# A new order for a diffusion backbone's first loads and first products

## The chip, the cores and the metric

The kernel runs on one core of a Trainium2 chip. A core has a matrix engine (TensorE, PE in the profile; its weight loads are listed as PEld), three engines for elementwise work (VectorE or DVE, ScalarE or ACT, GpSimd or POOL) and a sync engine (SyncE or SP), whose queue issues all loads and stores here. Each engine works through its own list of instructions in order, and they wait for one another through semaphores. The metric is the device time of one execution, in microseconds (us).

## The reference

Two layers over 1024 latent tokens of a 64-wide grid and 256 context tokens, all of width 1024, in float32. Each layer takes a modulation (shift, scale and gate for two halves of the layer) from a conditioning vector, normalizes and modulates the tokens, and mixes them. Cut to what the change touches, the head of layer 0:

```python
ml = (silu(c) @ w_mod[0] + b_mod[0]).reshape(B, 6, 1, D)      # for the latent tokens
mc = (silu(c_ctx) @ w_mod[0] + b_mod[0]).reshape(6, D)         # for the context tokens
hl = rms_norm(xl) * (1.0 + ml[:, 1]) + ml[:, 0]
hc = rms_norm(xc) * (1.0 + mc[1]) + mc[0]
pl, pc = hl @ w_in, hc @ w_in                                  # 1024 -> 1184 columns
```

Behind it come latent attention with low-rank queries and keys, a multi-scale pooling, an out-projection and a convolutional feed-forward; then layer 1 with grouped-query attention, its own feed-forward, and a last normalization of the latent stream.

## The kernel before, in words

Everything is held transposed: the feature on the 128 partitions, the token along the row. Tokens come in three chunks: 0 and 1 are the latent tokens 0 to 511 and 512 to 1023, chunk 2 the 256 context tokens. A chunk has eight feature tiles, k = 0 to 7. A product of accuracy near float32 is made from three products of a rounded high part and a low part (high x high, high x low, low x high), in mm3 (L72).

The head of the program, L505 to L708, is a region in which the order is written out by hand for all five engines: within one engine the instructions run in the order of the calls. It consists of small helpers that the change reorders:

- load_x(c) loads a chunk of tokens: eight tiles of 256 KB for chunks 0 and 1 (L445, L441), four for chunk 2 (L436). Tiles 0 to 3 of chunk 1 go into the buffers of chunk 0's tiles 0 to 3, and its tiles 4 to 7 into those of modulation weights that have been used.
- load_mod(n, half) loads eight tiles of 256 KB of the modulation's weights: n = 0 is the shift, n = 1 the scale; half 0 is feature tiles 0 to 3, half 1 is 4 to 7. g00, g10, g01 and g11 are (0,0), (1,0), (0,1) and (1,1).
- mod_rows(g) multiplies the conditioning vectors with one such half: eight float32 products of 512 columns on TensorE (L460), each two passes, then a copy of the resulting row on ScalarE (L462). mod_turn turns the row into columns with four tiny transposes on TensorE (L469), and two VectorE steps add the bias (L473).
- squares(xs, n) and add_squares: per tile a Square on ScalarE (L184 the first, L187 the others) and an addition on VectorE (L188); squares then splits the sum into a high part (ScalarE, L195) and a low part (VectorE, L196). total (L203, L204) adds them over the partitions on TensorE. newton makes the norm factor r of it: three steps of ScalarE (L167, L169, L170), and in the function that it returns three of VectorE (L173 to L175).
- scaled(c, k, r) multiplies a tile by r (VectorE, L477). high(c, k) makes the modulated high part on ScalarE (L487) and a float32 copy on GpSimd (L488), low_(c, k) the low part on VectorE (L489).
- getw(i) loads the i-th block of in-projection weights, 512 KB (L96); split(mt) makes its high part (GpSimd L117, or ScalarE L115) and its low part (VectorE, L111). The first three are blocks 4, 5 and 6, keys and part of the queries. The load buffers are two, and the first holds a row of srow until it is stored to d_sil.
- some(mt, c, k) is one call of mm3 for block mt, chunk c and tile k: three products. evac(mt, c) copies the finished sum out (ScalarE, L408).

So every engine's order in this stage is the order of these calls. Behind the region the buffers of the tokens are freed and the next stage begins (L907), written out by hand too except for SyncE. The change ends about halfway through the region; from high(2, 2) on they are the same.

Of the kernel before, what the change touches and what calls it, by code (L numbers as in the profile page):

```python
# [15 lines left out]
D = 1024  # L16
# [28 lines left out]
def backbone(tc, a):  # L45
# [161 lines left out]
    def rms_of(sq, n, width, tmp, psb, dst):  # L207

        newton(sq[0], total(sq, n, psb), n, width, tmp, dst)()
# [73 lines left out]
    def tables(name, pinned=True):  # L283

        i = S.preload_act_table_set(name)
        if pinned:
            tc.keep_in_program_order(i)
# [98 lines left out]
    def getw(i, **kw):  # L386
        if i < len(order) and order[i] not in win:
            win[order[i]] = wload(a["win0"][order[i]], **kw)

    def split(mt):  # L390
        if mt in win and callable(win[mt]):
            win[mt] = win[mt](mt not in (4, 5, 6), packed=mt == 9)

    prows = {}

# [33 lines left out]
    def load_x(c):  # L429
        c0, n = CH[c]  # L430
        xin[c] = []
        for k in range(8):
            if k % 2 == 0:
                if c == 2:
                    t2 = xp.tile([128, 512], F32, name="xin", tag="xin", bufs=4)
                    dma.dma_start(t2, a["xc"][:, k : k + 2, :])  # L436
                elif c == 0 or k < 4:
                    t2 = row(k // 2 % 2, name="xin")
            if c == 1 and k > 3:
                xin[c].append(hp.tile([128, 512], F32, name="xin", tag="h", bufs=40))  # L440
                dma.dma_start(xin[c][k], a["xl"][k, :, c0 : c0 + n])  # L441
                continue
            t = t2[:, k % 2 * n : k % 2 * n + n]
            if c < 2:
                dma.dma_start(t, a["xl"][k, :, c0 : c0 + n])  # L445
            xin[c].append(t)

    def load_mod(n, half):

        res = []  # L450
        for k in range(8):
            res.append(hp.tile([128, 512], F32, name="wn", tag="h", bufs=40))
            dma.dma_start(res[-1], a["wmodn"][n, half, k])
        return res

    def mod_rows(ws):

        b = psb("mod")[:2]
        for k in range(8):
            PE.matmul(b, scol[:, k, :], ws[k], start=k == 0, stop=k == 7)  # L460
        t = tmp("mrow", 512)[:2]
        S.copy(t, b)  # L462
        return t
# [11 lines left out]
    def scaled(c, k, r):  # L475

        V.tensor_mul(xin[c][k], xin[c][k], r)  # L477
# [24 lines left out]
    def low_(c, k):  # L502
        lows[c, k]()
# [8 lines left out]
    S.activation(scol, scol, AF.Silu)  # L512
    S.activation(srow, srow, AF.Silu)
    tables("natural_log_exp_and_others", False)
    g00 = load_mod(0, 0)
    load_x(0)
    g10 = load_mod(1, 0)
    dma.dma_start(d_sil, srow)
    dma.dma_start(ident, a["ident"])
    dma.dma_start(bmod, a["bmod"])  # L520
    r0 = tmp("r", 512)
    sq = squares(xin[0], 512, tmp, V)
    t0 = mod_rows(g00)
    g01 = load_mod(0, 1)
    rms_of(sq, 512, D, tmp, psb, r0)
    scaled(0, 3, r0)
    scaled(0, 7, r0)
    scaled(0, 0, r0)
    scaled(0, 5, r0)
    scaled(0, 1, r0)  # L530
    t1 = mod_rows(g10)
    getw(0)
    getw(1)
    mod_turn(0, 0, t0, 0.0)
    scaled(0, 6, r0)
    mod_turn(1, 0, t1, 1.0)
    g11 = load_mod(1, 1)
    high(0, 0)
    low_(0, 0)
    high(0, 1)  # L540
    split(4)
    split(5)
    scaled(0, 2, r0)
    low_(0, 1)
    high(0, 2)
    low_(0, 2)
    scaled(0, 4, r0)
    high(0, 3)
    low_(0, 3)
    t2 = mod_rows(g01)  # L550
    dma.dma_start(convw, a["convw"])
    some(4, 0, 0)
    some(4, 0, 1)
    getw(2, p=xp, tag="w", bufs=1)
    load_x(2)
    load_x(1)
    some(5, 0, 0)
    some(4, 0, 3)
    sq2 = squares(xin[2], 256, tmp, V)
    some(5, 0, 1)  # L560
    split(6)
    some(5, 0, 3)
    acc = add_squares(xin[1][:4], 512, tmp, V)
    mod_turn(0, 1, t2, 0.0)
    t3 = mod_rows(g11)
    some(5, 0, 2)
    r2 = tmp("r", 256)
    ss2 = total(sq2, 256, psb)
    rest2 = newton(sq2[0], ss2, 256, D, tmp, r2)
    r1 = tmp("r", 512)  # L570
    dma.dma_start(cols, a["cols"])
    some(6, 0, 0)
    mod_turn(1, 1, t3, 1.0)
    high(0, 5)
    high(0, 4)
    some(4, 0, 2)
    some(6, 0, 2)
    high(0, 7)
    some(6, 0, 1)
    low_(0, 5)  # L580
    some(6, 0, 3)
    some(4, 0, 5)
    low_(0, 4)
    some(5, 0, 4)
    rest2()
    high(0, 6)
    some(5, 0, 5)
    low_(0, 7)
    some(6, 0, 4)
    sq1 = squares(xin[1][4:], 512, tmp, V, acc)  # L590
    some(4, 0, 4)
    scaled(2, 7, r2)
    scaled(2, 5, r2)
    some(6, 0, 5)
    low_(0, 6)
    scaled(2, 6, r2)
    ss1 = total(sq1, 512, psb)
    some(6, 0, 6)
    scaled(2, 1, r2)
    rest1 = newton(sq1[0], ss1, 512, D, tmp, r1)  # L600
    high(2, 1)
    scaled(2, 4, r2)
    some(6, 0, 7)
    some(5, 0, 6)
    scaled(2, 2, r2)
    some(5, 0, 7)
    evac(6, 0, bk[6, 0])
    scaled(2, 0, r2)
    high(2, 0)
    rest1()  # L610
    evac(5, 0, bk[5, 0])
    some(4, 0, 6)
    some(4, 0, 7)
    high(2, 2)
    low_(2, 0)
    scaled(2, 3, r2)
# [2578 lines left out]
```

## Time and profile before

| What | Value |
|---|---|
| Runs | 2889.85 us median of 3 (2889.62 to 2891.6) |
| Profiled execution | 2893.38 us in all, span 2891.4 us |
| Granted TensorE clock over the span | 0.989 of full speed |
| TensorE busy, 40 to 50 us / 60 to 70 us / 80 to 90 us | 7.67 / 6.73 / 8.78 of 10 us |
| VectorE busy, 60 to 70 us | 8.94 of 10 us |
| ScalarE busy, 20 to 30 us / 30 to 40 us | 2.18 / 3.85 of 10 us |
| Bytes loaded, 10 to 20 us | 382 GB/s |

In a timeline each line is one instruction or several merged ones: start, time that they took together, engine, source line, operation, output<-input, sizes, count, and in brackets how long the engine sat idle before it and what ended that. The start and end of matrix products are modelled, so a product's listed time is longer than the step from one to the next. A row with 1.00 as clock (PEclk) had TensorE at full speed.

### The profile page before, as it was taken

To read this page: it belongs to the slowest core of one execution; us is meant where nothing else is said; L and a number is where in the kernel's file an instruction comes from. 1 tells how busy PE (TensorE), PEld (TensorE's weight loads), DVE (VectorE), ACT (ScalarE), POOL (GpSimd) and SP (SyncE) were. 2 spreads that over 40 slices of the span, in tenths; PEclk is the share of its full clock that TensorE was granted. 3 is DMA by queue.
4 is the path that set the end of the run, shared out by engine and by line. 5 is a ranking of instruction groups with operands and counts; after the bars stand their busy time and mean duration, and the time that the engine had idled before them with its cause. 6 is when DMAs were issued, how large, how long until landed. Compare 5 with 4: busy or idle time off the path is not lost.

```text
span 2891.4 us, 40143 instructions
## 1 busy us (share of the span) xinstructions
PE 2781.4 (96%) x14654; PEld 2316.9 (80%) x14654; DVE 2214.3 (77%) x3646; ACT 1240.3 (43%) x2520; POOL 1072.3 (37%) x1066
## 2 busy tenths in 40 slices
PE   7988999999999999999999998999999999999997
PEld 3857888887887888888888777999877788887886
DVE  5688888879887777778777887888757666559766
ACT  5525888824422333332002445888634333333104
POOL 2242444762243455431012443444331445452112
PEclk9999999999999999999999999999999999999998
DMA  6144001283144343363221010000131222226311
GB/s 229 70 141 139 15 24 58 81 277 110 55 130 127 108 137 128 131 209 125 73 72 49 31 37 23 1 1 1 37 138 44 81 88 73 85 93 228 98 59 59
DMA packets 97229, 264.89 MB, mean 92 GB/s; under 512 B 11908, under 2 KB 21060, under 8 KB 96904
## 3 DMA queue, kind: packets, MB, share of 16 engines
q1 hardware_dynamic: 97032, 262.33, 27.1%
q8 instruction: 115, 1.88, 0.3%
q14 instruction: 82, 0.67, 0.1%
HBM read 212.53 MB, written 49.75 MB: 91 GB/s over the span
## 4 chain that ended last, share of the span: by engine, by line
PE 58%; DVE 10%; ACT 3%; issue 2%; DMA 1%; POOL 1%; DVEq 0%; SPq 0%; ACTq 0%; POOLq 0%
PE d L72 18%; PE y L72 9%; PE x L72 6%; PE z L72 6%; PE p L72 5%; PE pv L1277 3%; PE b L72 3%; PE T L1264 2%; PE S L1197 1%; PE S L1199 1%; PE S L1198 1%; PE qk L72 1%; DVE x L2009 1%; DVE x L2008 1%; DMA wm<-in_wmod 1%
## 5 line engine op out<-in xcount | busy, mean ns | idle before, releaser
L2091 DVE SCALAR_TENSOR_TENSOR x<-d,mod,x 128x512 f32<-128x512 f32 (+1 forms) x352 | 254.5, 735 | 94.8 <-PE d L72 92.5
L1246 POOL TENSOR_SCALAR p<-p,sm 128x1280 f32<-128x1280 f32 x128 | 171.4, 1339 | 287.9 <-DVE sm L1245 190.2
L1267 DVE TENSOR_TENSOR tl<-T,th 128x512 fp32r<-128x512 f32 x328 | 225.5, 688 | 46.8 <-ACT th L1266 41.8
L1277 PE MATMUL pv<-th,v 128*128 128x256 f32 x976 | 254.1, 309 | 1.4 <-ACT vo L1406 1.0
L1220 DVE TENSOR_REDUCE mx<-S 128x1 f32<-128x512 f32 (+1 forms) x400 | 233.9, 585 | 11.0 <-PE S L1199 3.7
L72 PE MATMUL d<-act,wh 128*128 128x512 f32 (+1 forms) x832 | 231.9, 365 | 0.0
L1266 ACT CAST th<-T 128x512 fp32r<-128x512 f32 x328 | 192.1, 586 | 84.5 <-PE T L1264 77.2
L2074 ACT CAST act<-act 128x512 fp32r<-128x512 f32 (+1 forms) x110 | 61.3, 577 | 382.2 <-PE d L72 259.8
L72 PE MATMUL b<-h,wh 128*128 128x512 f32 (+1 forms) x752 | 206.6, 362 | 6.0 <-DVE h L489 4.1
L1694 POOL TENSOR_TENSOR x<-raw 128x512 f32<-128x512 f32 x80 | 114.5, 1432 | 237.2 <-DMA raw<-in_wup 158.7
L72 PE MATMUL x<-h,a1h 128*128 128x512 f32 x624 | 197.7, 398 | 2.5 <-ACT a1h L1676 2.5
L1264 PE MATMUL T<-ident,p 128*128 128x128 f32 x1280 | 193.0, 272 | 1.5 <-POOL p L1246 1.5
L1975 ACT COPY su<-x 128x512 f32<-128x512 f32 x40 | 23.4, 586 | 381.4 <-PE x L72 348.7
L1264 PEld LDWEIGHTS T<-ident,p 128*128 128x128 f32 x1280 | 156.5, 140 | 34.9 <-POOL p L1246 3.2
L1277 PE MATMUL pv<-tl,v 128*128 128x256 f32 x656 | 177.3, 282 | 0.0
L1277 PEld LDWEIGHTS pv<-th,v 128*128 128x128 f32 x976 | 173.4, 189 | 2.4 <-ACT vo L1406 1.5
L72 PEld LDWEIGHTS d<-act,wh 128*128 128x128 f32 x832 | 149.5, 189 | 27.2
L2015 POOL TENSOR_TENSOR su<-x,su 128x512 f32<-128x512 f32 x78 | 140.5, 1813 | 79.5 <-DVE su L1997 67.0
L72 PEld LDWEIGHTS b<-h,wh 128*128 128x128 f32 x752 | 133.0, 189 | 36.0 <-DVE h L489 5.4
L72 PE MATMUL d<-act,wl 128*128 128x512 f32 (+1 forms) x416 | 151.9, 365 | 0.0
L72 PEld LDWEIGHTS x<-h,a1h 128*128 128x128 f32 x624 | 118.6, 190 | 30.3 <-ACT a1h L1676 2.9
L1237 ACT ACTIVATE p<-S,mx,rq 128x512 f32<-128x512 f32 (+1 forms) x192 | 136.2, 712 | 12.6 <-DVE mx L1228 11.1
(515 smaller groups left out, 8185.0 us busy)
## 6 DMA issues: line engine op xcount, KB each, us to landing
raw<-in_wup SPq DMA_DIRECT2D x86, 512.0 KB, 3.3
wm<-in_wmod SPq DMA_DIRECT2D x72, 512.0 KB, 3.6
act<-d_act SPq DMA_DIRECT2D x88, 256.0 KB, 3.5
raw<-in_wdn SPq DMA_DIRECT2D x44, 512.0 KB, 4.3
raw<-in_wout SPq DMA_DIRECT2D x32, 512.0 KB, 3.4
d_act<-su SPq DMA_DIRECT2D x22, 640.0 KB, 3.4
d_act<-su SPq DMA_DIRECT2D x22, 512.0 KB, 2.9
raw<-in_win SPq DMA_DIRECT2D x20, 512.0 KB, 3.5
```

What stands on the lines that cost most here:

```text
L72: PE.matmul(out, w, x, start=first and i == 0, stop=last and i == n - 1, skip_group_check=more)
L1220: V.reduce_max(mx[:, j : j + 1], s, axis=AX.X)
L1237: S.activation(o, s, AF.Exp, scale=self.scale, bias=self.mx[:, 3:4], accum_out=self.sm[:, j : j + 1])
L1246: P.tensor_scalar(out=self.p, in0=self.p, scalar1=sm[:, 3:4], scalar2=1.0, op0=ALU.mult, op1=ALU.mult)
L1264: PE.transpose(tb[:, (2 * j + i) * 128 : (2 * j + i) * 128 + 128], rows[i].p[:, c : c + 128], ident)
L1266: S.copy(hi, tb)
L1267: V.tensor_sub(lo, tb, f32(hi))
L1277: PE.matmul(out[0], st, mv, start=(u + j == 0 and x == 0), stop=(u + j == n - 1 and x == len(ops) - 1))
L1694: eng.tensor_tensor(out=t, in0=self.src(f, x), in1=self.src(f, y), op=op)
L2015: eng.tensor_mul(self.s_of(c), self.t[c], self.s_of(c) if u is None else u)
L2074: S.copy(hi, f32(lo))
L2091: V.scalar_tensor_tensor(out=x, in0=b, scalar=mod[self.l, c // 2][:, 40 + d : 41 + d], in1=x, op0=ALU.mult, op1=ALU.add)
```

## The change

The loads come in another order: the tokens of chunk 0 first, then g00, three small ones, g10, two blocks of weights, and g01; before it was g00, the tokens, g10, the small ones, g01, the weights. The sum of squares of chunk 0 is multiplied out behind the first row product, and only two of its tiles are scaled ahead of the weights' splits. Block 5 is split on ScalarE instead of GpSimd. The products of blocks 4 and 5 with tiles 0 to 3 all come ahead of the row products of g01 and g11, which now follow each other, with the turn of the first inside the second. The squares of chunks 2 and 1 come behind these. The last products of chunk 0 go tile by tile.

```diff
--- before.py
+++ after.py
@@ -389,7 +389,7 @@
 
     def split(mt):
         if mt in win and callable(win[mt]):
-            win[mt] = win[mt](mt not in (4, 5, 6), packed=mt == 9)
+            win[mt] = win[mt](mt not in (4, 6), packed=mt == 9)
 
     prows = {}
 
@@ -453,11 +453,13 @@
             dma.dma_start(res[-1], a["wmodn"][n, half, k])
         return res
 
-    def mod_rows(ws):
+    def mod_rows(ws, between=None):
 
         b = psb("mod")[:2]
         for k in range(8):
             PE.matmul(b, scol[:, k, :], ws[k], start=k == 0, stop=k == 7)
+            if between and k == 2:
+                between()
         t = tmp("mrow", 512)[:2]
         S.copy(t, b)
         return t
@@ -512,105 +514,105 @@
     S.activation(scol, scol, AF.Silu)
     S.activation(srow, srow, AF.Silu)
     tables("natural_log_exp_and_others", False)
+    load_x(0)
     g00 = load_mod(0, 0)
-    load_x(0)
-    g10 = load_mod(1, 0)
-    dma.dma_start(d_sil, srow)
     dma.dma_start(ident, a["ident"])
     dma.dma_start(bmod, a["bmod"])
-    r0 = tmp("r", 512)
+    dma.dma_start(d_sil, srow)
+    g10 = load_mod(1, 0)
+    getw(0)
+    getw(1)
+    g01 = load_mod(0, 1)
     sq = squares(xin[0], 512, tmp, V)
     t0 = mod_rows(g00)
-    g01 = load_mod(0, 1)
-    rms_of(sq, 512, D, tmp, psb, r0)
-    scaled(0, 3, r0)
-    scaled(0, 7, r0)
+    r0 = tmp("r", 512)
+    ss0 = total(sq, 512, psb)
+    mod_turn(0, 0, t0, 0.0)
+    newton(sq[0], ss0, 512, D, tmp, r0)()
+    t1 = mod_rows(g10)
     scaled(0, 0, r0)
-    scaled(0, 5, r0)
     scaled(0, 1, r0)
-    t1 = mod_rows(g10)
-    getw(0)
-    getw(1)
-    mod_turn(0, 0, t0, 0.0)
-    scaled(0, 6, r0)
+    split(4)
+    split(5)
     mod_turn(1, 0, t1, 1.0)
+    getw(2, p=xp, tag="w", bufs=1)
     g11 = load_mod(1, 1)
     high(0, 0)
     low_(0, 0)
     high(0, 1)
-    split(4)
-    split(5)
     scaled(0, 2, r0)
     low_(0, 1)
+    some(4, 0, 0)
+    some(5, 0, 0)
     high(0, 2)
+    scaled(0, 3, r0)
     low_(0, 2)
-    scaled(0, 4, r0)
+    some(4, 0, 1)
+    some(5, 0, 1)
     high(0, 3)
+    scaled(0, 5, r0)
     low_(0, 3)
-    t2 = mod_rows(g01)
-    dma.dma_start(convw, a["convw"])
-    some(4, 0, 0)
-    some(4, 0, 1)
-    getw(2, p=xp, tag="w", bufs=1)
     load_x(2)
     load_x(1)
-    some(5, 0, 0)
+    dma.dma_start(convw, a["convw"])
+    dma.dma_start(cols, a["cols"])
+    some(4, 0, 2)
+    some(5, 0, 2)
     some(4, 0, 3)
+    some(5, 0, 3)
+    split(6)
+    t2 = mod_rows(g01)
+    scaled(0, 4, r0)
+    scaled(0, 7, r0)
+    scaled(0, 6, r0)
+    t3 = mod_rows(g11, lambda: mod_turn(0, 1, t2, 0.0))
     sq2 = squares(xin[2], 256, tmp, V)
-    some(5, 0, 1)
-    split(6)
-    some(5, 0, 3)
     acc = add_squares(xin[1][:4], 512, tmp, V)
-    mod_turn(0, 1, t2, 0.0)
-    t3 = mod_rows(g11)
-    some(5, 0, 2)
+    some(6, 0, 0)
+    some(6, 0, 1)
+    mod_turn(1, 1, t3, 1.0)
     r2 = tmp("r", 256)
     ss2 = total(sq2, 256, psb)
     rest2 = newton(sq2[0], ss2, 256, D, tmp, r2)
     r1 = tmp("r", 512)
-    dma.dma_start(cols, a["cols"])
-    some(6, 0, 0)
-    mod_turn(1, 1, t3, 1.0)
+    some(6, 0, 2)
+    some(6, 0, 3)
     high(0, 5)
     high(0, 4)
-    some(4, 0, 2)
-    some(6, 0, 2)
+    low_(0, 5)
+    some(4, 0, 5)
+    some(5, 0, 5)
+    some(6, 0, 5)
+    high(0, 6)
+    low_(0, 4)
+    rest2()
+    some(4, 0, 4)
+    some(5, 0, 4)
+    some(6, 0, 4)
     high(0, 7)
-    some(6, 0, 1)
-    low_(0, 5)
-    some(6, 0, 3)
-    some(4, 0, 5)
-    low_(0, 4)
-    some(5, 0, 4)
-    rest2()
-    high(0, 6)
-    some(5, 0, 5)
+    low_(0, 6)
+    scaled(2, 1, r2)
+    scaled(2, 0, r2)
+    sq1 = squares(xin[1][4:], 512, tmp, V, acc)
+    some(6, 0, 6)
+    some(4, 0, 6)
+    some(5, 0, 6)
     low_(0, 7)
-    some(6, 0, 4)
-    sq1 = squares(xin[1][4:], 512, tmp, V, acc)
-    some(4, 0, 4)
+    scaled(2, 2, r2)
     scaled(2, 7, r2)
-    scaled(2, 5, r2)
-    some(6, 0, 5)
-    low_(0, 6)
-    scaled(2, 6, r2)
+    some(6, 0, 7)
+    evac(6, 0, bk[6, 0])
     ss1 = total(sq1, 512, psb)
-    some(6, 0, 6)
-    scaled(2, 1, r2)
+    some(5, 0, 7)
     rest1 = newton(sq1[0], ss1, 512, D, tmp, r1)
     high(2, 1)
+    evac(5, 0, bk[5, 0])
+    high(2, 0)
+    scaled(2, 5, r2)
+    scaled(2, 6, r2)
     scaled(2, 4, r2)
-    some(6, 0, 7)
-    some(5, 0, 6)
-    scaled(2, 2, r2)
-    some(5, 0, 7)
-    evac(6, 0, bk[6, 0])
-    scaled(2, 0, r2)
-    high(2, 0)
+    some(4, 0, 7)
     rest1()
-    evac(5, 0, bk[5, 0])
-    some(4, 0, 6)
-    some(4, 0, 7)
     high(2, 2)
     low_(2, 0)
     scaled(2, 3, r2)
```

## The prediction

> **What bounds the kernel now.** I read the page first. TensorE (PE) is busy nearly all the time, so time is won or lost where it waits, and the change touches the first 99 us alone.
>
> ```profile
> span 2891.4 us, 40143 instructions
> ...
> PE 2781.4 (96%) x14654; PEld 2316.9 (80%) x14654; DVE 2214.3 (77%) x3646; ACT 1240.3 (43%) x2520; POOL 1072.3 (37%) x1066
> ```
>
> I then read the stretch 0 to 100 us engine by engine in the timeline, and there the idle column. What I call a row product is one call of mod_rows (L456), which gives a half of the shift or the scale as a row: R00 and R10 are the first halves of shift and scale, R01 and R11 the second halves. First those four and the first product of the weights:
>
> ```profile
> 4.87 9.95 PE L460 MATMUL mod<-wn,scol 128*2 128x512 f32 x16 [4.87 <-ACT scol L512]
> ...
> 20.36 9.03 PE L460 MATMUL mod<-wn,scol 128*2 128x512 f32 x16
> ...
> 30.73 7.03 PE L460 MATMUL mod<-wn,scol 128*2 128x512 f32 x16
> 37.69 0.73 PE L72 MATMUL b<-h,wh 128*128 128x512 f32 x2
> ...
> 45.02 7.03 PE L460 MATMUL mod<-wn,scol 128*2 128x512 f32 x16
> ```
>
> The first column is the start, the second how long the merged group lasted. The four row products cost 9.95, 9.03 and twice about 7.03 us (R11 begins at 45.02); the fourth row is the first product with real weights, at 37.69. Weight products come in threes (one call of some, L493), and a call takes 0.70 us, from one wl row to the next:
>
> ```profile
> 42.96 0.39 PE L72 MATMUL b<-h,wl 128*128 128x512 f32 x1
> 43.19 0.63 PE L72 MATMUL b<-h,wh 128*128 128x512 f32 x2
> 43.66 0.40 PE L72 MATMUL b<-h,wl 128*128 128x512 f32 x1
> ```
>
> After R11 come two waits for the squares of chunk 1's tokens, and then, near the end of the stage, this one for the last modulated tokens:
>
> ```profile
> 85.15 0.51 PE L72 MATMUL b<-h,wh 128*128 128x512 f32 x1 [1.22 <-DVE h L489]
> ```
>
> From there TensorE runs without a gap into the next stage, whose work follows the last products at about 98.4, when ScalarE takes the last two sums out:
>
> ```profile
> 98.50 1.07 ACT L408 COPY low<-b 128x512 f32<-128x512 f32 x2 [1.14 <-PE b L72]
> ```
>
> So the stage ends as much after 85.15 as its remaining products take, and 85.15 is set by VectorE (DVE) and GpSimd (POOL), which make the low parts (L489) in one unbroken chain:
>
> ```profile
> 54.27 0.23 DVE L473 SCALAR_TENSOR_TENSOR mod<-turn,bmod 128x4 f32<-128x4 f32 x2 [3.26 <-PE turn L469]
> 55.42 0.69 DVE L489 TENSOR_TENSOR h<-z,h 128x512 fp32r<-128x512 f32 x1 [0.92 <-POOL z L488]
> ...
> 60.13 3.07 DVE L188 TENSOR_TENSOR x<-x,y 128x512 f32<-128x512 f32 x4
> 63.89 0.69 DVE L196 TENSOR_TENSOR lo<-x,hi 128x512 fp32r<-128x512 f32 x1 [0.68 <-ACT hi L195]
> 64.50 0.75 DVE L477 TENSOR_TENSOR xin<-xin,r 128x256 f32<-128x256 f32 x2
> ...
> 69.99 0.41 DVE L489 TENSOR_TENSOR h<-z,h 128x256 fp32r<-128x256 f32 x1
> ```
> ```profile
> 70.50 8.29 POOL L488 TENSOR_SCALAR z<-xin,mod 128x256 f32<-128x256 f32 x8 [0.97 <-DVE h L489]
> ```
>
> The low parts of the context tokens start at 69.99, right after the norm factor r of chunk 1 is done, and the eight GpSimd steps behind them follow each other from 70.50 without a hole. The code behind that point is the same before and after. **So I look for one number: when that first low part of chunk 2 (69.99 before) comes after the change.** The end of the stage follows it one for one.
>
> **The change, step by step.** Loads first. The queue issues one 256 KB load per 0.675 us (5.40 / 8), and the first of the second group of eight lands at 11.42:
>
> ```profile
> 5.28 5.40 SPq L445 DMA_DIRECT2D xin<-in_xl  x8
> ...
> 5.78 1.28 ACT L285 ACT_TABLE_LOAD   x1
> ...
> 11.42 0.63 ACT L184 ACTIVATE x<-xin 128x512 f32<-128x512 f32 x1 [4.36 <-DMA xin<-in_xl]
> ...
> 18.24 0.62 ACT L195 CAST hi<-x 128x512 fp32r<-128x512 f32 x1 [0.96 <-DVE x L188]
> ```
>
> After the change that place belongs to the first-half modulation g00, while the tokens take the place of 4.87. So R00 starts at 11.4, not 4.87. The squares of chunk 0 now run beside it and are hidden: one at a time they need the 6.8 us between 11.42 and the cast of their sum at 18.24, and can start when the table load ends at 7.06, so they are done by about 15. R00 takes 9.95 (its own cold row): end 21.4. The sum of squares and the turn of R00 on TensorE, 0.9 together, lead to 22.4, and R10 runs straight on, at 7.03 since TensorE does not go idle before it as it did from 14.8 to 18.9: end **29.4**, exactly where it was (29.39). The chain of the norm factor (from the first step of ScalarE to the last of VectorE 4.2 us, rows below) ends at 26.1 and two scaled calls at 27.4, both ahead of that.
>
> ```profile
> 20.47 0.69 ACT L167 ACTIVATE x<-ss,epst 128x512 f32<-128x512 f32 x1 [1.14 <-PE ss L204]
> ```
> ```profile
> 23.96 0.69 DVE L175 SCALAR_TENSOR_TENSOR r<-x,r 128x512 f32<-128x512 f32 x1
> ```
>
> Now the weights. split(5) has moved its cast from GpSimd to ScalarE (ACT), and it stands behind the copy of R10's row there, while its subtraction stands ahead of mod_turn(1, 0) on VectorE. The rows for these steps:
>
> ```profile
> 29.77 0.57 ACT L462 COPY mrow<-mod 2x512 f32<-2x512 f32 x1 [7.29 <-PE turn L469]
> 31.04 1.52 ACT L487 ACTIVATE h<-xin,mod 128x512 fp32r<-128x512 f32 x2 [0.69 <-DVE mod L473]
> ```
> ```profile
> 94.77 1.05 ACT L115 CAST wh<-raw 128x1024 fp32r<-128x1024 f32 x1 [4.37 <-PE b L72]
> ```
> ```profile
> 31.95 0.71 DVE L489 TENSOR_TENSOR h<-z,h 128x512 fp32r<-128x512 f32 x1 [0.88 <-POOL z L488]
> ```
> ```profile
> 46.96 0.43 DVE L196 TENSOR_TENSOR lo<-x,hi 128x256 fp32r<-128x256 f32 x1 [0.47 <-ACT hi L195]
> 47.45 1.22 DVE L111 TENSOR_TENSOR wl<-raw,wh 128x1024 fp32r<-128x1024 f32 x1
> 48.59 2.28 DVE L188 TENSOR_TENSOR x<-x,y 128x512 f32<-128x512 f32 x3
> ```
>
> Copy 0.57, cast 1.05, subtraction 1.22, two tiny modulation steps 0.23, high and z beside each other 0.82, low part 0.70: 29.4 + 4.6 = 34.0, a little over it with the gaps; first weight product at **34.1** (37.69 before). TensorE idles 3.7 us ahead of it. Then k = 0 to 3 for weights 4 and 5: VectorE gives a low part every 1.4 us (one scaled, one low, 0.69 each), two calls take 1.4, so eight calls end at 34.1 + 5.65 = 39.8. R01 and R11 with a turn between them: 39.8 + 7.03 + 7.03 + 0.45 = **54.3** (52.05 before). At that point the change has eight calls done instead of six, so TensorE alone is 2.2 us later and 1.4 us richer: nearly even.
>
> The squares decide. Before, the squares of the context tokens came on ScalarE ahead of the copy of R11's row:
>
> ```profile
> 42.13 0.42 ACT L184 ACTIVATE x<-xin 128x256 f32<-128x256 f32 x1 [2.13 <-DMA xin<-in_xc]
> ...
> 52.09 0.57 ACT L462 COPY mrow<-mod 2x512 f32<-2x512 f32 x1 [2.15 <-PE mod L460]
> ```
>
> They started on landing (42.13), and the copy followed at 52.09. The change puts both groups of squares (sq2 and acc) behind mod_rows(g11), so behind that copy in ScalarE's order. All that ScalarE issues stands behind it: 12 squares, a cast, three steps of r2, all high calls of k = 4 to 7. From 37 to 54 ScalarE has only the copy of R01. The squares now start at 54.9, 12.8 us later:
> - sq2 to its lo: 47.39 - 42.13 = 5.3, so 60.2. TensorE reaches ss2 at 56.1 and waits 4 us.
> - acc: three additions at 0.76, the first at about 60.9, end 63.1.
> - mod_turn(1, 1) on VectorE is queued behind these additions: 63.4 instead of 54.5, though its transposes are done by 56.1. High and low of k = 5 (from 54.51 to 56.11 before, 1.6): 65.2. TensorE, out of work at 61.9, waits 3.3 us more.
> - From the end of that low part to the end of the lo of chunk 1's squares: 64.58 - 56.11 = 8.5 before, and now two short scaled calls more (0.75): **74.4**.
> - low_(0, 7) has moved from ahead of those additions to behind them (0.65), and some(6, 0, 7) stands ahead of ss1 (0.70), which takes 0.55: ss1 done at 76.4.
> - From the end of ss1 (65.13) to 69.99 there were 4.86 us; 0.5 off, as two VectorE steps of r1 were stretched to 0.93 by GpSimd, which now has nothing to do there: **81.1**.
>
> ```profile
> 64.63 0.50 PE L204 MATMUL ss<-lo,ones 128*128 128x512 f32 x1 [0.23 <-DVE lo L196]
> ```
>
> So the sum is 81.1 - 70.0 = 11.1 us later, and the stage ends at about 109.5 instead of 98.4.
>
> Costs taken as nothing. R01 and R11 find their loads there: getw(2) waits on SP's queue for the subtraction of weight 4 (28.6), g11 behind it is issued by 35 and lands by 41 (landing took up to 6.7 us), R11 needs it at 46.8; x(2) and x(1) behind those land by 44 and 49, and are used from 54.9 on. With that cover gone every microsecond of lateness would count. convw and cols are small and used in the next stage. getw(1) reuses the buffer of srow and must wait for d_sil, which now goes out seven microseconds ahead of it. The edits in the order of the calls at k = 4 to 7 cost what is listed; the rest lies on engines that wait.
>
> What the trace of before does not show: the clock of TensorE after the new gaps. Rows with the granted clock:
>
> ```profile
> 17.00:18.00 1.00, 0.00 (x0) 0.00 (x0) 0.90 (x2) 0.28 (x1) 0.00 (x0) 0.80 1.04 383
> 24.00:25.00 1.00, 1.00 (x3) 0.14 (x2) 0.97 (x2) 0.00 (x0) 0.00 (x0) 0.78 0.94 342
> 65.00:66.00 1.00, 0.46 (x3) 0.10 (x1) 1.00 (x3) 0.80 (x2) 0.00 (x0) 0.70 0.00 0
> 68.00:69.00 1.00, 1.00 (x4) 0.77 (x4) 0.97 (x2) 0.56 (x2) 1.00 (x2) 0.60 0.00 0
> ```
>
> It fell at 17.6 after TensorE stopped at 14.8, and came back at 24.4; fell again at 65.4 and came back at 68.8. At half clock a call of some takes 1.4 instead of 0.7. So the gap at 30.4 to 34.1 costs between 0 and 3.4 us / 2 = 1.7, as R00 may be between 0 and 1.7 cheaper, since both sizes depend on when the clock is granted: in the two cold starts of before, 5.9 and 5.5 us of work went by. I take nothing for either, and keep 9.4 to 12.8 for the two. The later gaps (56 to 60, 62 to 65) fall beside the chain of VectorE, and the nine calls behind 65.2 still end at 74.3 at half clock for 5.9 us, just ahead of 75; only some(6, 0, 7) and ss1 could add 1.
>
> [...]
>
> The profiled execution of before took 2893.38 us in all for a span of 2891.4; the runs have a median of 2889.85. I add the difference to the median: 2889.85 + 11.1 = **2901**.
>
> **Rivals.**
> 1. *The clock falls in every gap*: 11.1 + 1.7 + 1.0 = 13.8, 2903.7. For it: both long idles of before brought it down. Against: the shorter wait at 85.15 did not, and most of the gaps lie beside VectorE's chain.
> 2. *Part of it is given back later*: TensorE has idle time after the stage (the row below, 6.3 of 10 us busy), and if what it waits for there doesn't shift, up to half of the 11 us would vanish: +5.5, 2895.4. Against: nearly all engines follow a written order from stage to stage, and the next loads wait for the buffers that this stage frees.
>
> ```profile
> 170.00:180.00 10.00, 6.26 (x27) 4.45 (x25) 6.89 (x10) 4.49 (x10) 3.74 (x2) 0.90 0.44 122
> ```
>
> 3. *The squares do not wait*: if sq2 ran as its tokens land (44), ss2 would be met at 56, the low part of k = 5 would end at 58.2, and the same steps would give 73.4, +3.4 us, 2893.3: no change that can be told. Against: ScalarE kept its order before, where the copy of R10 waited 7.29 us.
> 4. *Faster: TensorE never waits after 34.1.* From there it has 8 calls, two row products, 16 calls of chunk 0, 24 of half the width at 0.35, 24 at 0.70 and 2 us of small things: 58 us, so the stage would end at 92.2, 6.2 us sooner than 98.4, 2883.6. It decides itself at ss2: the squares of the context tokens must start by 50.8. For it: TensorE's own sum is shorter by the cold clock it no longer meets at R10. Against: the copy of R11 at 54.3 alone breaks it.
>
> **How the numbers follow.** The forecast with its clock bounds (9.4 to 12.8) has 0.50, rival 1 0.23, rival 2 0.15, rival 3 0.06, rival 4 0.06. What can be told from no change is about 0.2% (5.8 us): slower needs more than 2895.6. Forecast and rival 1 lie above, and some two thirds of rival 2, which runs from 0 given back to half and more: 0.83 slower, 0.11 within, 0.06 faster. The range leaves out rivals 3 and 4 and the tail of rival 2 and reaches 1.8 over rival 1 for errors of step lengths: 2893.5 to 2905.5. The forecast's own range is 2899 to 2903.
>
> **What would show it right or wrong.** R00 starting near 11.4, R10 ending near 29.4, a first weight product near 34; the first square of the context tokens right behind the copy of R11 and not before 50; a wait of TensorE of some 4 us for lo at ss2; the first low part of chunk 2 near 81 and the stage's last copies near 109. Squares of the context tokens at 44, or R11 ending before 48, would make it wrong; so would a low part of chunk 2 at 81 with the end of the program not following.

## The result, and the profile after

The changed kernel takes 2907.03 us (median of 5 runs, 2904.7 to 2909.58), the kernel before beside it 2891.29 us (5 runs, 2889.62 to 2894.88). The ratio is 1.0051, with a 95% interval of 1.0039 to 1.0062: slower by 15.7 us by the medians. The prediction was 2901.0, with 2893.5 to 2905.5 as its range, so the sign is right and the time is 6 us too low, 1.5 beyond the range. The profiled execution took 2908.43 us, against 2893.38 for that of before.

The head of the page, span and busy times:

```profile
span 2906.5 us, 40145 instructions
...
PE 2785.9 (96%) x14654; PEld 2320.2 (80%) x14654; DVE 2213.1 (76%) x3646; ACT 1243.4 (43%) x2521; POOL 1073.7 (37%) x1065
```

TensorE worked 4.5 us more than before (2781.4), with the same 14654 products, and the span is 15.1 us longer: the rest is waiting. TensorE's timeline of the first stage follows; in brackets the idle time ahead of a row and what ended it.

```profile
11.60 9.96 PE L460 MATMUL mod<-wn,scol 128*2 128x512 f32 x16 [11.60 <-DMA wn<-in_wmodn]
...
22.55 7.03 PE L460 MATMUL mod<-wn,scol 128*2 128x512 f32 x16
...
33.46 0.48 PE L72 MATMUL b<-h,wh 128*128 128x512 f32 x1 [2.81 <-POOL z L490]
...
51.55 4.45 PE L460 MATMUL mod<-wn,scol 128*2 128x512 f32 x10
...
61.84 0.56 PE L203 MATMUL ss<-hi,ones 128*128 128x256 f32 x1 [3.90 <-ACT hi L195]
```

R00 starts at 11.60, R10 at 22.55, the first weight product at 33.46 after an idle time of 2.81 us, and R11 ends at 56.00. Behind it TensorE waits 3.90 us for the squares of the context tokens. ScalarE's timeline shows why:

```profile
56.10 0.57 ACT L464 COPY mrow<-mod 2x512 f32<-2x512 f32 x1 [6.72 <-PE mod L460]
56.58 0.41 ACT L184 ACTIVATE x<-xin 128x256 f32<-128x256 f32 x1
```

ScalarE had idled for 6.72 us when the copy of R11's row let it go on; the first square stands right behind that copy, at 56.58, not at 42.13. VectorE's timeline, with the step that the prediction made its one number, and the row that ends the stage:

```profile
81.90 0.42 DVE L491 TENSOR_TENSOR h<-z,h 128x256 fp32r<-128x256 f32 x1
```

```profile
110.42 1.07 ACT L408 COPY low<-b 128x512 f32<-128x512 f32 x2 [1.14 <-PE b L72]
```

The first low part of chunk 2 comes at 81.90 (69.99 before) and the stage ends 28.52 us later; before, these two rows were 28.51 us apart. So the stage is 11.92 us longer. The forecast said 11.1. That leaves 3.2 us of the span (15.1) that do not come from the stage. They arise mainly in one place, the first product of the attention scores. The last product ahead of it starts 12.77 us later than before (277.10 against 264.33), but the third product of the third group of score products, the last row of each view below, 16.37 us later. Behind it 1.3 us come off again by the end. TensorE's timeline there, before:

```profile
264.33 0.39 PE L72 MATMUL b<-wh,low 128*128 128x512 f32 x1
264.56 0.40 PE L1197 MATMUL S<-k0h,q0h 96*128 96x512 f32 x1
...
268.98 0.28 PE L1199 MATMUL S<-k0h,q0l 96*128 96x256 f32 x1
```

And after, with the vector engine's rows of the value parts:

```profile
277.10 0.39 PE L72 MATMUL b<-wh,low 128*128 128x512 f32 x1
279.30 0.47 PE L1199 MATMUL S<-k0h,q0h 96*128 96x512 f32 x1 [1.81 <-issue]
...
285.35 0.28 PE L1201 MATMUL S<-k0h,q0l 96*128 96x256 f32 x1
```

```profile
277.02 3.40 DVE L1298 TENSOR_TENSOR v<-b,v 128x256 fp32r<-128x256 f32 x10
```

Before, the score product (S) follows the last value product (b) 0.23 us later. After, TensorE sits idle for 1.81 us, and "issue" means that the profile names nothing for which it waited. The windows behind it, with the granted clock in the column ahead of the last two (those are the share of the transfers and their GB/s):

```profile
280.00:282.00 2.00, 2.00 (x7) 1.52 (x7) 1.01 (x3) 0.00 (x0) 0.00 (x0) 0.59 0.00 0
282.00:284.00 2.00, 2.00 (x7) 1.57 (x6) 0.69 (x3) 0.65 (x2) 0.00 (x0) 0.56 0.00 0
```

By these two rows the clock was at half for some 3.4 us, from 280.4 to 283.8. From the end of the stage on the order of the instructions is the same in both kernels, on every engine; something else must differ.

### The profile page after: what moved, and what is told of

Same layout as the page of the kernel before. It is cut to its first block, busy times and chain, and to the rows that moved or that the text cites. A ratio compares the mean times of both kernels' runs of the same rounds, so it can differ in the third digit from the quotient of the medians.

```text
span 2906.5 us, 40145 instructions
## 1 busy us (share of the span) xinstructions
PE 2785.9 (96%) x14654; PEld 2320.2 (80%) x14654; DVE 2213.1 (76%) x3646; ACT 1243.4 (43%) x2521; POOL 1073.7 (37%) x1065
## 4 chain that ended last, share of the span: by engine, by line
PE 56%; DVE 11%; ACT 3%; issue 2%; DMA 1%; POOL 1%; DVEq 0%; SPq 0%; ACTq 0%; POOLq 0%
PE d L72 18%; PE y L72 8%; PE x L72 6%; PE z L72 6%; PE p L72 5%; PE pv L1279 3%; PE b L72 3%; PE T L1266 2%; PE qk L72 1%; PE S L1199 1%; DVE x L2011 1%; PE S L1201 1%; PE S L1200 1%; DVE x L2010 1%; DMA wm<-in_wmod 1%
```

## The experiments

Two questions, each with its rivals. What makes the stage longer: the order of the products, above all the squares of the context tokens behind the copy of R11's row (the prediction's own reason), or the loads, since R00 starts 6.7 us later? And what makes the wait at the score product: the accumulator bank that it is given, or the delay as such, by its phase against the clock or the transfers? The expectations name theories by letters, and each says what its letters stand for (L is one theory in e6 and e7 and another in e10 and e11). All of the kernels ran beside runs of before. "Stage end" is the start of the row with the last two sums in the profiled execution, and "S wait" the idle time ahead of the first score product.

| Kernel | Median, us (runs) | Ratio to before, 95% interval | Stage end, us | S wait, us |
|---|---|---|---|---|
| before | 2891.29 (5) | | 98.50 | none |
| after | 2907.03 (5) | 1.0051 [1.0039, 1.0062] | 110.42 | 1.81 |
| e1 squares first | 2897.69 (6) | 1.0030 [1.0019, 1.0042] | 104.16 | 1.76 |
| e2 split on GpSimd | 2903.81 (5) | 1.0050 [1.0037, 1.0064] | 108.29 | 2.23 |
| e3 ss1 earlier | 2907.11 (5) | 1.0062 [1.0049, 1.0075] | 110.75 | 1.95 |
| e4 before + 7 us | 2901.09 (5) | 1.0034 [1.0021, 1.0046] | 105.62 | none |
| e6 before, turn moved | 2895.0 (11) | 1.0012 [1.0004, 1.0021] | 96.88 | 2.24 |
| e7 after, turn moved | 2904.69 (5) | 1.0052 [1.0038, 1.0065] | 110.22 | none |
| e8 three undone | 2897.6 (9) | 1.0028 [1.0018, 1.0038] | 104.34 | none |
| e9 and g00 first | 2898.51 (6) | 1.0028 [1.0016, 1.0039] | 105.01 | none |
| e10 loads alone | 2888.37 (11) | 0.9995 [0.9986, 1.0004] | 98.11 | none |
| e11 products alone | 2908.4 (5) | 1.0057 [1.0044, 1.007] | 112.83 | 2.24 |
| e12 row in gap | 2890.09 (11) | 0.9998 [0.9989, 1.0007] | 98.07 | none |

**e1, the squares first.**

```diff
 after
+    sq2 = squares(xin[2], 256, tmp, V)
+    acc = add_squares(xin[1][:4], 512, tmp, V)
     t2 = mod_rows(g01)
...
     t3 = mod_rows(g11, lambda: mod_turn(0, 1, t2, 0.0))
-    sq2 = squares(xin[2], 256, tmp, V)
-    acc = add_squares(xin[1][:4], 512, tmp, V)
```

> The changed kernel with both groups of squares (sq2 and acc) called ahead of mod_rows(g01) instead of behind mod_rows(g11). Theory A (the squares behind the copy of R11's row set the delay): the first square of the context tokens at 40 to 42 us instead of 56.6, no wait of TensorE at ss2, the first low part of k = 5 at about 60.8 instead of 66.3, the first low part of chunk 2 at about 76.4 instead of 81.9, the total 5.5 us below the changed kernel. Theory B (the cold clock and the weights' split set it, the squares lie beside them): the squares move, but the first low part of chunk 2 stays within 1 us of 81.9 and the total too.

ScalarE of e1, the first square and the two rows' copies:

```profile
38.41 0.42 ACT L184 ACTIVATE x<-xin 128x256 f32<-128x256 f32 x1 [2.79 <-DMA xin<-in_xc]
...
47.76 0.57 ACT L464 COPY mrow<-mod 2x512 f32<-2x512 f32 x1 [1.55 <-PE mod L460]
55.11 0.57 ACT L464 COPY mrow<-mod 2x512 f32<-2x512 f32 x1 [6.78 <-PE mod L460]
```

The square starts as its tokens land, 18 us earlier than in after, and both copies come behind it. TensorE has no wait at ss2 any more. The stage ends 6.26 us earlier than after's:

```profile
104.16 1.07 ACT L408 COPY low<-b 128x512 f32<-128x512 f32 x2 [1.14 <-PE b L72]
```

Not all of this is the edit. R01, up to which TensorE's order is the same, already starts 1.0 us earlier (40.69 against 41.69), since R00 took 8.36 us in this execution and 9.96 in after's. So the squares' place is worth some 5.3 us of the stage. Against the runs of before beside each, e1 is 8.7 us longer and after 14.7 (ratios 1.0030 and 1.0051), so e1 is 6 us shorter; the medians differ by 9.3, but the runs of before beside them differ by 2.0 too.

**e2, block 5 split on GpSimd as before.**

```diff
 after
-            win[mt] = win[mt](mt not in (4, 6), packed=mt == 9)
+            win[mt] = win[mt](mt not in (4, 5, 6), packed=mt == 9)
```

> The changed kernel with block 5's cast back on GpSimd, as before. Theory A: the modulation's first half is ready at 30.7 instead of 32.3 us, the first weight product comes 1.6 us sooner, and the total falls by 1.6; if the shorter idle time also keeps the clock up, by 1.9 more, 3.5 in all. Theory C (this step lies beside something else): the first weight product moves, the first low part of chunk 2 and the total do not (within 0.5).

TensorE of e2, the first row product and the first weight product:

```profile
11.73 8.62 PE L460 MATMUL mod<-wn,scol 128*2 128x512 f32 x16 [11.73 <-DMA wn<-in_wmodn]
...
31.38 0.47 PE L72 MATMUL b<-h,wh 128*128 128x512 f32 x1 [1.93 <-POOL z L490]
```

The first weight product comes 2.08 us earlier than after's 33.46, but 1.2 of that was there when R10 started (21.35 against 22.55), as R00 took 8.62 us this time and 9.96 in after, with the same 16 passes. What the cast costs on ScalarE is the 0.9 us by which TensorE's idle time shrank (2.81 to 1.93). The intervals of the two ratios overlap, so the runs tell no more than that it is small.

**e3, the sum of chunk 1's squares earlier.**

```diff
 after
+    low_(0, 7)
     sq1 = squares(xin[1][4:], 512, tmp, V, acc)
...
-    low_(0, 7)
...
+    ss1 = total(sq1, 512, psb)
     some(6, 0, 7)
     evac(6, 0, bk[6, 0])
-    ss1 = total(sq1, 512, psb)
```

> The changed kernel with low_(0, 7) ahead of the last squares' additions and ss1 ahead of some(6, 0, 7), as before. Theory A: the sum of squares of chunk 1 ends 1.3 us sooner, the first low part of chunk 2 at 80.6 instead of 81.9, the total 1.3 lower. Theory C: under 0.5, as VectorE has the same work ahead of it.

Nothing was won. ScalarE of e3 behind ss1:

```profile
77.57 0.59 ACT L408 COPY low<-b 128x512 f32<-128x512 f32 x1 [2.00 <-PE b L72]
78.05 0.70 ACT L167 ACTIVATE x<-ss,epst 128x512 f32<-128x512 f32 x1
```

ss1 itself came 1 us earlier, but ScalarE has the copy of block 6's sum ahead of the norm factor's first step (L167), and that copy waits for some(6, 0, 7), which was only moved behind ss1. So the prediction's charge for ss1's later place was no cost of its own: the copy ends last there. The stage ended 0.33 us later than after's.

**e4, a pure delay.** The row product of g11 is made twice in the kernel before, and the first result is dropped.

```diff
 before
     mod_turn(0, 1, t2, 0.0)
+    mod_rows(g11)
     t3 = mod_rows(g11)
```

> The kernel before with the row product of g11 made twice (the first result is not used): a pure delay of 7.03 us at 52 us, with no other order changed. Theory A (the end of the program follows the end of the first stage one for one): the stage ends 7.0 us later and the total is 7.0 above the kernel before. Theory D (a shift of the later stages costs by itself, as their waits meet the clock otherwise): the stage ends 7.0 later, the total is 9 to 11 above.

The stage ends 7.12 us later, the profiled execution (2899.11 us) is 5.7 us longer, and the ratio's interval is 6.1 to 13.3 us. So the end of the program follows the stage. One for one (theory A) lies near the lower end of the interval and theory D's 9 to 11 us in its middle, so whether a late stage costs something more by itself stays open. TensorE of e4 at the score product:

```profile
271.98 0.40 PE L72 MATMUL b<-wh,low 128*128 128x512 f32 x1
272.22 0.40 PE L1198 MATMUL S<-k0h,q0h 96*128 96x512 f32 x1
```

No wait: a late stage alone doesn't bring it. So the cause is elsewhere. The built program's instruction list gives for that product, beside its transfers:

```
before  waits for  DVE: y <- b, cols, x            (an output product of the stage ahead)
after   waits for  DVE: v <- b, v                  (the third of the five value parts)
e4      waits for  DVE: k1l <- b, k1h              (a key part)
```

In this kernel the products' sums lie in a pool of eight accumulator banks (psb, L376). It gives each new sum a bank that is free, so each later sum's bank depends on the order of all earlier ones. The score products have a pool of their own (L1304 of after), whose first sum takes bank 0. In before bank 0 last held an output sum that is long read out; in after it holds the third value product, and VectorE is done reading that with the sixth of the ten subtractions that begin at 277.02: 277.02 + 6 x 0.34 = 279.06. The score product starts at 279.30. The row says "issue" where the list has the wait. The packed trace also holds the semaphore instructions that the rows leave out. In after, one of TensorE's that waits for VectorE's semaphore and for a load that had landed at 275.01 ends at 279.13, 0.03 us behind VectorE's signal at 279.10. All six kernels in which the score product waits (S wait in the table) show the same, with 0.04 us at most between the signal and the end of the wait.

**e6 and e7, the bank alone.** One line's place decides: where the turn of g01's row stands to the row product of g11. Each of the two takes a bank from the pool (L458 and L469), so swapping them swaps two places in the pool's order. No work is added or taken.

```diff
 before (e6)
-    mod_turn(0, 1, t2, 0.0)
     t3 = mod_rows(g11)
+    mod_turn(0, 1, t2, 0.0)
 after (e7)
-    t3 = mod_rows(g11, lambda: mod_turn(0, 1, t2, 0.0))
+    mod_turn(0, 1, t2, 0.0)
+    t3 = mod_rows(g11)
```

> Kernel before, with one line moved: the transposes of the row g01 (mod_turn(0, 1)) come after the row product of g11 instead of ahead of it. No work is added. Among the PSUM banks it changes which bank each later product gets: the first score product, whose bank is bank 0, then follows on the third of the five last value products (as in the kernel after) instead of on an earlier output product (as in the kernel before). Theory B (bank): stage 1 ends within 0.5 us of before's 98.50, the first score product, which had no wait at 264.56, waits 1.8 to 2.2 us for the vector engine's v<-b subtraction, a slow clock window costs another 1.7, and the kernel is 3.5 us longer than before: ratio 1.0012. Theory L (the later 3.5 us of the kernel after come from where its stage 1 ended, that is from the phase of the clock windows or of the transfers): no wait at the score product, 0 to 0.5 us longer, ratio 1.0000 to 1.0002.

> Kernel after, with the same line moved the other way: the transposes of the row g01 stand ahead of the row product of g11, not after its third step. No work is taken away. The first score product's bank then follows on an output product that is long done, as in the kernel before. Theory B (bank): the first score product starts without its wait of 1.81 us and the slow window behind it is gone, -3.5 us; the transposes wait for the copy of the row, up to +0.9 us in stage 1; together 2.6 to 3.5 us less than the kernel after: 2903.5 to 2904.5. Theory L: nothing changes after stage 1, 0 to 0.9 us more than after: 2907 to 2908.

e6 at the score product, TensorE and then VectorE:

```profile
262.45 0.40 PE L72 MATMUL b<-wh,low 128*128 128x512 f32 x1
265.08 0.76 PE L1197 MATMUL S<-k0h,q0h 96*128 96x512 f32 x1 [2.24 <-issue]
```

```profile
262.81 3.39 DVE L1296 TENSOR_TENSOR v<-b,v 128x256 fp32r<-128x256 f32 x10
```

The wait is there in a kernel that is otherwise before: 2.24 us, and again the product starts 0.23 us after VectorE's sixth subtraction (262.81 + 6 x 0.34 = 264.85). e6's ratio of 1.0012 is 3.5 us (1.2 to 6.1), as the bank's theory gave. The stage of the profiled execution ended 1.62 us earlier than before's, though, and not within 0.5 of it as expected: R00 took 8.94 us there and 9.95 in before. e7 at the same place:

```profile
278.40 0.40 PE L72 MATMUL b<-wh,low 128*128 128x512 f32 x1
278.64 0.40 PE L1200 MATMUL S<-k0h,q0h 96*128 96x512 f32 x1
```

The wait is gone, 0.24 us from the value product to the score product. e7's median is 2.3 us below after's, but its ratio to before (1.0052) is no lower than after's (1.0051), where 2.6 to 3.5 us less had been expected. So the runs of e7 show no gain; that the wait is gone is shown by its row alone. The stretch from the start of the last value product to that of the third product in the third group of scores (4.65 us in before, 8.25 in after) gives the price over all traces, and e6's runs agree with it. Six kernels with the wait: 7.14 to 10.09 us, mean 8.46. Seven without: 4.64 to 5.72, mean 5.15. So 3.3 us, of which the wait is some 2 and the rest mostly a clock at half behind it.

**e8 and e9, undoing more.** e8 is e1 with e2's and e7's edits; e9 also loads g00 ahead of the tokens.

```diff
 e8 (e9)
-    load_x(0)
     g00 = load_mod(0, 0)
+    load_x(0)
```

> Kernel after with three parts undone: the context squares ahead of the last row products (as in e1), the split of weight 5 on GpSimd (as in e2) and the transposes ahead of the row product of g11 (as in e7). If the three costs are separate: e1's 2897.7, less 2.1 (e2's stage end) and less 2.6 to 3.5 (e7) gives 2892 to 2893. If they share one cause, or if the squares' gain needs the transposes where they were: 2895 to 2898.

> As e8, and the first row's weights g00 are loaded ahead of the tokens, as in the kernel before, so that the first row product starts at 4.87 us instead of 11.6. If the late start of the first row product is what still separates e8 from before: 3 to 6 us less than e8, 2887 to 2889. If the row of tokens' squares, which now end some 4 us later, only takes its place ahead of ss0 and the second row product: 0 to 1.5 us less than e8, 2891 to 2893.

The costs do not add up. e8 is as long as e1 (2897.6 and 2897.69). ScalarE and TensorE of e8:

```profile
40.07 0.42 ACT L184 ACTIVATE x<-xin 128x256 f32<-128x256 f32 x1 [5.02 <-DMA xin<-in_xc]
...
44.46 0.40 ACT L195 CAST hi<-x 128x256 fp32r<-128x256 f32 x1 [0.64 <-DVE x L188]
...
47.21 0.56 ACT L464 COPY mrow<-mod 2x512 f32<-2x512 f32 x1
```

```profile
47.82 0.40 PE L471 MATMUL turn<-ident,mrow 2*128 2x2 f32 x4 [1.26 <-ACT mrow L464]
...
69.62 0.78 PE L72 MATMUL b<-h,wh 128*128 128x512 f32 x1 [2.59 <-DVE h L491]
```

The earlier first product only meets the next wait: the context tokens land at 40, so both groups of squares run until 47, the copy of R01's row comes after them, and the turn, now ahead of R11, waits for that copy (1.26 us; 0.72 in e7, which has no squares ahead of the copy). Behind it the same waits for low parts (2.59 at 69.62) are left. The bank's 3.3 us should still have come off. In the traces they do: from the end of the stage to the third product in the third group of scores e8 takes 171.45 us and e1 174.85. The runs don't show it, but the intervals (5.5 to 12.1 us over before for e1, 5.2 to 11.0 for e8) leave room for it. In e9 R00 starts at 4.87, yet its first weight product comes at 32.54 and its runs are no shorter than e8's:

```profile
4.87 8.91 PE L460 MATMUL mod<-wn,scol 128*2 128x512 f32 x16 [4.87 <-ACT scol L514]
18.83 0.72 PE L203 MATMUL ss<-hi,ones 128*128 128x512 f32 x1 [5.04 <-ACT hi L195]
...
32.54 1.51 PE L72 MATMUL b<-h,wh 128*128 128x512 f32 x2 [1.19 <-POOL z L490]
```

The tokens now land behind g00, so ss0 waits 5.04 us for the squares. Whichever of the two is loaded first, the other sets when R10 can start (with the tokens first, in after, R00 waits for its weights until 11.60).

**e10 and e11, the halves of the change.** e10 has the new first loads and the old order of products; e11 the reverse.

```diff
 before (e10)
-    g00 = load_mod(0, 0)
     load_x(0)
-    g10 = load_mod(1, 0)
-    dma.dma_start(d_sil, srow)
+    g00 = load_mod(0, 0)
     dma.dma_start(ident, a["ident"])
     dma.dma_start(bmod, a["bmod"])
+    dma.dma_start(d_sil, srow)
+    g10 = load_mod(1, 0)
+    getw(0)
+    getw(1)
+    g01 = load_mod(0, 1)
...
-    g01 = load_mod(0, 1)
...
-    getw(0)
-    getw(1)
```

> One half of the change alone: the loads in the new order (tokens, g00, constants, g10, the first two weights, g01), the products in the old one. Score product's bank as in before. Theory P (the order of the products costs the time, the loads do not): R00 starts at 11.4 instead of 4.87 but ends by 21.4, where before's second row product had to wait for its weights until 29.4 anyway; R10 and R01 follow without a gap, R01 ends near 36.5 instead of 37.7, the first weight product starts there, and the stage ends 1 us earlier to 0.5 later than before's 98.50: ratio 0.9997 to 1.0002. Theory L (the late start of the first row product costs the time): the 6.5 us carry through, ratio 1.002.

> The other half alone: the products in the new order, the loads in the old one (g00, tokens, g10, constants, g01, weights). Score product's bank as in after. Theory P: R00 at 4.87, R10 ends near 29.4 as in before, but the weights land as late as in before, so the first weight product starts at 35.5 to 37.7 with TensorE idle for 5 to 7 us ahead of it (R01 no longer stands there); the squares of the context tokens start as late as in after; the stage ends 2 to 4 us later than after's 110.42, and the score product waits as in after: 2909 to 2911. Theory L: with the old loads most of the loss is gone, 2893 to 2896.

TensorE of e10:

```profile
11.66 9.77 PE L460 MATMUL mod<-wn,scol 128*2 128x512 f32 x16 [11.66 <-DMA wn<-in_wmodn]
...
22.02 7.03 PE L460 MATMUL mod<-wn,scol 128*2 128x512 f32 x16
...
37.34 0.73 PE L72 MATMUL b<-h,wh 128*128 128x512 f32 x2
```

R00 starts 6.8 us later than in before, and the first weight product 0.35 us earlier. In before R10 ended at 29.39 (20.36 + 9.03) in spite of its early R00; here it ends at 29.05. The ratio's interval holds 1 and ends 1.2 us above it, so no cost of the loads is seen. TensorE of e11:

```profile
4.87 9.30 PE L460 MATMUL mod<-wn,scol 128*2 128x512 f32 x16 [4.87 <-ACT scol L514]
...
35.02 1.51 PE L72 MATMUL b<-h,wh 128*128 128x512 f32 x2 [2.81 <-POOL z L490]
```

With the old loads and the new products the stage ends at 112.83, later than after's, and the score product waits, as its bank said it would. TensorE idles 2.81 us ahead of the first weight product, where 5 to 7 had been expected. So the order of the products costs the time and the loads do not: by the stage ends the new loads even win back 2.4 us of what the new order of products loses, though the runs of e11 and after cannot be told apart.

**e12, the row product back in the gap.** e1, and the row product of g01 ahead of the first weight products, as before has it; its turn ahead of g11's.

```diff
 e1
+    t2 = mod_rows(g01)
     some(4, 0, 0)
     some(5, 0, 0)
...
-    t2 = mod_rows(g01)
...
-    t3 = mod_rows(g11, lambda: mod_turn(0, 1, t2, 0.0))
+    mod_turn(0, 1, t2, 0.0)
+    t3 = mod_rows(g11)
```

> As e1 (kernel after with the context squares ahead of the last row products), and the row product of g01 put back ahead of the first weight products, where the kernel before has it; its transposes stand ahead of the row product of g11, so that the score product's bank is free early. Theory P (the new order of the products costs the time by two moves: the squares behind both row products, and no row product to cover the making of the first pieces): TensorE works from 30.6 to 37.6 instead of waiting 2.8 us and then running the first products at half clock for some 3.4 us; the stage ends 3 to 5 us earlier than e1's 104.16, at 99 to 101, and the score product does not wait: 2889.5 to 2893. Rival (what is left in e1 is the order of the pieces and additions behind 60 us, which stays as in after): the stage ends at 103 to 104.5, and only the score product's 3.5 us go: 2894 to 2895.

TensorE of e12, then the windows of 20 to 40 us in e1 and in e12:

```profile
29.65 7.03 PE L460 MATMUL mod<-wn,scol 128*2 128x512 f32 x16
...
42.73 7.03 PE L460 MATMUL mod<-wn,scol 128*2 128x512 f32 x16
```

```profile
20.00:40.00 20.00, 16.52 (x48) 8.28 (x49) 13.87 (x20) 8.31 (x13) 7.56 (x6) 0.83 1.02 373
```

```profile
20.00:40.00 20.00, 19.33 (x59) 6.26 (x58) 13.21 (x19) 8.66 (x14) 7.95 (x6) 1.00 1.00 355
```

R01 runs where e1 waited. In e1 the clock fell to 0.83 over these 20 us, as TensorE idled ahead of the first weight products and then made them at half rate (0.50 in each of the windows 32 to 34, 34 to 36 and 36 to 38); in e12 it stays at 1.00, and 2.8 us more of the window are worked. The stage ends 6.09 us earlier than e1's, at before's own end (98.50), and the kernel is as fast as before (ratio 0.9998):

```profile
98.07 1.07 ACT L408 COPY low<-b 128x512 f32<-128x512 f32 x2 [1.14 <-PE b L72]
```

So two moves account for the 11.92 us of the stage, since undoing both takes all of it back: the squares behind the row products, and no row product over the making of the first pieces. Each is worth 5 to 7 us; by the stage ends they are 6.26 and 6.09, but 1.0 of the first is R00's shorter time in e1. None of the versions is shown to beat the kernel before; e10 and e12 equal it.

## Why the prediction was wrong, point by point

- *R00 near 11.4, R10 ending near 29.4, a first product near 34*: 11.60, 29.58 and 33.46. Right.
- *Eight calls end at 39.8*: R01 began at 41.69. The clock, costed at nothing with 1.7 kept as its bound, fell: TensorE idled 2.81 us ahead of the first product, and the windows show 0.65 and 0.50 there. Half clock for 3.4 us (34.6 to 38.0) is the bound of 1.7, so this term was mis-sized. A call took 1.28 us there (from 35.74 to 37.02, wl row to wl row), and not the forecast's 1.4.

```profile
34.00:36.00 2.00, 1.81 (x5) 1.48 (x6) 2.00 (x4) 0.84 (x2) 1.29 (x2) 0.65 0.97 325
36.00:38.00 2.00, 2.00 (x6) 1.52 (x6) 1.40 (x3) 0.82 (x1) 2.00 (x2) 0.50 1.03 392
```

- *Squares behind the copy, at 54.9, a wait of 4 us at ss2, first low part near 81.1*: 56.58, 3.90 and 81.90. The mechanism was right, and e1 shows it. The squares came 1.7 us later than forecast, as R01 had, and 0.9 of that was gone at the first low part. Part of this is no gain: the forecast's own steps from ss1 on, 76.4 + 4.86 - 0.5, give 80.8 and not 81.1, so its sum should have been 10.8 and not 11.1.
- *The stage's end follows the first low part one for one*: 28.52 us after, 28.51 before. Right.
- *The code behind is the same, and the end of the program follows*: this is the step that failed. The code is the same but not the banks. The new order of sums in the first stage put the first score product on a bank that was still being read, some 169 us behind the end of the stage, and added 1.81 us of wait and the half clock behind it, 3.6 us in these two traces (4.65 and 8.25 us over the stretch named with e7). Stage 11.92 and this 3.6 make 15.5, against 15.7 by the medians; that they meet so closely is partly luck, as the other differences behind the stage in these two traces, 0.85 and -1.3, nearly cancel. No rival had it, and the range reached 1.8 us over its highest case for step lengths alone. The forecast's own last sign of being wrong came true, a low part near 81 with the end of the program not following. Of the 6.0 us by which it missed, 3.6 are this step, 0.8 the stage, and 1.4 the base: it added its sum to a median of 2889.85, and before ran at 2891.29 beside the changed kernel. Without the 3.6 the time would have lain within the range.
- *Rival 1, the clock falls in every gap, 2903.7*: it did fall, and windows show it at 0.50 from 61.9 to 65.3 and from 68.8 to 72.1 too. But the later two lay beside VectorE's chain, and the stage's measured sum was 11.92, not its 13.8. That 13.8 with the bank's 3.6 would come to 2907.3, the measured time, is luck.
- *Rival 2, given back later*: no. e4's delay of 7.12 us was 6.1 to 13.3 us in its runs, and after's own delay stood at 15.1 us at the end of its trace.
- *Rival 3, squares that don't wait, 2893.3*: not this kernel, but e1 made it so. Its stage was 5.66 us late and not 3.4, as the first weight products still ran at half clock (0.50 from 32 to 38), and the score product's wait of 1.76 us came on top: 2897.7.
- *Rival 4, faster*: no; e12 shows how much of TensorE's idle time the old places of R01 and the squares had covered.

What stays open: whether a late stage costs something by itself (e4), and why the runs of e7 and e8 show nothing of the bank's 3.3 us, which their traces show. The scatter is of this size. Runs of before alone spread from 2884.68 to 2895.14 us, and traces of kernels with the same code between stage end and the last value product differ by up to 2.9 us there (165.28 in e11, 168.18 in e7), so single traces cannot settle 1 to 2 us. Farther on they drift more: e10 is 0.3 us ahead of before at the scores and 6.7 at the end of the span.

## What to carry to other kernels

Where a long product waits for nothing but its loads (a row product here), it is cover, worth 6.09 us of the stage in e12: before moving it, look at what TensorE would wait for in its old place, and put nothing that others wait for, such as squares (some 5.3 us of the stage in e1), behind its copy in another engine's order. A change of order in one stage can move later accumulator banks (in e6 one line's place brought a wait of 2.24 us), so compare the waits of the built programs behind the change too, not the order of instructions alone. The load that started late cost nothing in e10 (R00 6.8 us later, the first weight product 0.35 us earlier), as the work behind it was waiting for another load anyway.

## What the hardware showed that I had not expected

The same wait had very different prices. In e6 and in e11 the score product waited 2.24 us, but over the stretch named with e7 e6 took 10.09 us and e11 7.14. Windows of e6 and of e11 behind the wait:

```profile
264.50:265.00 0.50, 0.00 (x0) 0.00 (x0) 0.50 (x3) 0.00 (x0) 0.00 (x0) 0.76 0.85 168
...
268.00:271.00 3.00, 3.00 (x8) 2.33 (x8) 1.03 (x3) 0.65 (x2) 0.00 (x0) 0.50 0.00 0
271.00:272.00 1.00, 1.00 (x4) 0.78 (x4) 0.33 (x1) 0.00 (x0) 0.00 (x0) 0.71 0.00 0
```

```profile
280.00:282.00 2.00, 1.25 (x6) 1.07 (x7) 2.00 (x7) 0.00 (x0) 0.00 (x0) 1.00 0.37 106
282.00:284.00 2.00, 2.00 (x10) 1.64 (x9) 0.67 (x2) 0.65 (x2) 0.00 (x0) 1.00 0.00 0
```

In e6 the clock was at half from 264.8 to 271.6, and in e11 it did not move (in after it lay between: half for 3.4 us). The 6.8 us of e6 are twice the 3.4 us of after, and before has a stretch of either length in its first stage: 6.8 us from 17.6 to 24.4 and 3.4 us from 65.4 to 68.8. TensorE was not idle for all of the 3.4 us ahead of 264.8: it had worked until 262.85, for some 1.5 us of them, and the clock fell all the same. So here idle time of under 2 us was enough; what share of work keeps the clock up, these runs do not settle, as in e11 the clock stayed at 1.00 through the same wait of 2.24 us.

R00, TensorE's first work and the same 16 passes in each kernel, took 8.36 us in e1, 8.62 in e2, 8.94 in e6 and 9.96 in after, where the 16 passes of R10 took 7.03. So R00's time alone can move the first weight product by up to 1.6 us.
